# Feed-forward as two layers per token half, the second also in seven half products

## The chip, the cores and the metric

The kernel runs on one core of one Trainium2 chip. The metric is the device time of one execution in microseconds (us); several executions are given by their median. The engines are named as the profile names them: PE (matmuls) with its weight loads PEld, DVE, ACT, POOL, and SP, whose queue issues most of the DMAs.

## The reference

One decoder layer on 2048 tokens of width 1024: a token mixer (stick-breaking attention and gated DeltaNet, unchanged here) and then a feed-forward part, all in float32:

```python
h = rmsnorm(x, norm_mlp[l]) * (1.0 + sc_m) + sh_m
x = x + g_m * (jnp.square(jax.nn.relu(h @ w_ff1[l])) @ w_ff2[l])
```

w_ff1 is 1024 x 4096, w_ff2 is 4096 x 1024. The scale, the shift and the gate g_m come from a conditioning vector.

## The kernel before

Everything is kept transposed: features on the 128 partitions, tokens in the free dimension. Each float32 product is made of three matmuls in the reduced type fp32r: an operand is split into a high part (a rounding copy on ACT) and a low part (operand minus high part, a subtraction on DVE or POOL), and high x high, high x low and low x high are summed in PSUM. A left operand's parts are called wh and wl (swh and swl in the first feed-forward layer), with three buffers each.

After the mixer, project_out makes the mixer's output product for 512 tokens (a chunk) at a time and writes x1, the residual stream, to DRAM; outs(2), then outs(1, 0) are the last calls. load_h(1) stands between them: it loads x1 of the second half of the tokens (chunks 2 and 3), normalizes and modulates it, and makes the right operands of the first feed-forward layer. These lie in pool fb on the right side of SBUF, four tiles of each kind. load_h(0) makes those of the other half.

The first layer, ff1(hf, g), makes 256 features (group g of 16) for one half of the tokens (1024 tokens, hf). It is a 2 x 2 block product over halves of the input features, of the 256 features and of the 1024 tokens, done by seven block products in place of eight (Strassen's scheme in Winograd's form). Each of the seven has 4 matmul steps of 128 input features and three matmuls per step: 84 in all. summed makes the four sums or differences of weight blocks on POOL, product splits a left operand and multiplies, take copies a partial result from PSUM (ACT), add adds one from PSUM (DVE) and applies relu and the square (ACT). load_h makes the sums on the right side once per half of the tokens, into the tiles b0, b12, b56 and b43 (bh for high, bl for low parts).

split then splits the features, and ff2(hf, g, hid, ys) multiplies them with the 256 matching rows of w_ff2, in the plain way: 8 output tiles x 2 feature tiles x 2 token chunks x 3 = 96 matmuls. Each of the 16 PSUM tiles of 128x512 is evicted by one scalar_tensor_tensor (L1181) that multiplies with g_m and adds to the accumulator ys in SBUF. So the loop alternates: ff1 of group g+1 is issued ahead of ff2 of group g. A loop turn is 84 + 96 matmuls, and there are 32 turns (2 halves x 16 groups). At the last group but one of the first half, load_h(0) is issued with high priority.

PSUM has 8 banks in this stage: four with tag f1 for the first layer and four with tag f2 for the second. All engines run their instructions in a fixed order, which a planner sets beforehand: it simulates the engines, starts what is ready by priority, and gives buffers of a pool to whichever tile asks first in that simulation. tc.high_priority moves instructions ahead. DMAs of the SP queue are issued in that fixed order too, and one that waits for its buffer holds back those behind it.

Of the kernel before, what the change touches and what calls it, by code (L numbers as in the profile page):

```python
# [56 lines left out]
def tile_hybrid_layer(  # L57
# [74 lines left out]
    if True:  # L132
# [883 lines left out]
        ADD, SUB = ALU.add, ALU.subtract  # L1016
        fb = right.enter_context(tc.tile_pool(name="fb", bufs=4, side="right", reuse_waits="tile"))

        def load_h(hf, pair, rs):

            out = [[] for _ in range(7)]
            for k in range(4):
                bt = {}
                for j, shape in (("0", [P, CH]), ("12", b2_), ("56", b2_), ("43", b2_)):
                    bt[j] = [fb.tile(shape, F32R, tag=f"b{i}{j}", name=f"b{i}{hf}_{k}{j}") for i in "hl"]
                b = []
                for i in range(2):
                    kk = k + 4 * i
                    x = pair(f"fx{hf}_{kk}")
                    for n in range(2):  # L1030
                        nc.sync.dma_start(x[:, n], x1_d[2 * hf + n][:, kk, :])
                    for n in range(2):
                        V.tensor_tensor(x[:, n], x[:, n], rs[n], ALU.mult)  # L1033
                    A.activation(x, x, AF.Identity, scale=g2[:, kk:kk + 1], bias=mods[:, 24 + kk:25 + kk])
                    b.append(x)

                def parts2(j, x):
                    hi, lo = bt[j]
                    A.copy(hi, x)
                    lo_part(lo, x, hi)  # L1040

                x1, x2 = b
                parts2("0", x1[:, 0])
                parts2("12", x2)
                G.tensor_tensor(x1[:, 0], x1[:, 1], x1[:, 0], SUB)
                G.tensor_tensor(x1[:, 1], x2[:, 1], x1[:, 1], SUB)
                parts2("56", x1)
                G.tensor_tensor(x2[:, 1], x2[:, 1], x1[:, 0], SUB)
                G.tensor_tensor(x2[:, 0], x2[:, 1], x2[:, 0], SUB)  # L1049
                parts2("43", x2)  # L1050
                out[0].append(bt["0"])
                for j, (key, i) in enumerate((("12", 0), ("12", 1), ("43", 0), ("56", 0), ("43", 1), ("56", 1))):
                    out[j + 1].append([t[:, i] for t in bt[key]])
            return out
# [235 lines left out]
```

## Time and profile before

| what | value |
|---|---|
| runs, median (lowest to highest) | 2884.83 us (2874.47 to 2891.14) |
| the profiled execution | 2880.04 us, its span 2878.2 us |
| PE busy, share of the span | 93% |
| DVE, ACT, POOL busy | 67%, 44%, 30% |
| mean granted clock | 0.966 of full speed |

The busy times are sums over a span with several stages: mixer first, feed-forward from about 1520 us to the end. Line numbers (L1176) are those of the kernel printed above; names such as swh are the tiles' names without their numbers. PE's matmuls overlap in the records, so one is shown longer (about 0.39 us) than the distance from start to start.

### The profile page before, as it was taken

The page shows a single profiled execution, that of the slowest core. Times are in us where ns is not written, and L with a number is a line of the kernel's source. Part 1 is how long each engine was busy: PE and PEld are TensorE (multiplying, and loading weights), DVE is VectorE, ACT ScalarE, POOL GpSimd, SP SyncE. Part 2 cuts the span into 40 slices and gives each one's busy share as a digit, 9 for nine tenths or more (in the row PEclk, how much of TensorE's full clock was granted, in tenths as well). Part 3 has the DMA queues.
Part 4 walks back from the last instruction along what each step waited for, and adds up shares of the span by engine and source line. Part 5 has one row for each costly group of instructions (what it writes and reads, how often), then busy time and mean ns, then how long its engine had stood idle before and what let it go on. Part 6 is the DMA issues. An engine that isn't in the chain of part 4 may idle for free.

```text
span 2878.2 us, 37573 instructions
## 1 busy us (share of the span) xinstructions
PE 2684.7 (93%) x13044; PEld 2144.3 (75%) x13044; DVE 1933.6 (67%) x4355; ACT 1264.1 (44%) x2488; POOL 873.7 (30%) x686
## 2 busy tenths in 40 slices
PE   3998889789999899989989999999998999999999
PEld 2786667667787677866667888888876888888887
DVE  7487889695775968676685555556568556555555
ACT  4553444444553456535454433343345443344332
POOL 3333313241322523132264222222235222222221
PEclk9998999899999999999999999999999999999999
DMA  7443675343344444336463111111125111111012
GB/s 249 158 149 107 195 240 193 93 130 130 120 149 126 153 135 151 116 88 194 137 199 131 59 46 43 59 59 40 49 86 177 59 59 35 54 59 59 30 59 88
DMA packets 184612, 321.17 MB, mean 112 GB/s; under 512 B 22216, under 2 KB 69320, under 8 KB 180296
## 3 DMA queue, kind: packets, MB, share of 16 engines
q1 hardware_dynamic: 167368, 291.20, 31.4%
q10 hardware_dynamic: 17024, 27.27, 2.6%
q8 instruction: 110, 1.80, 0.3%
q14 instruction: 110, 0.90, 0.1%
HBM read 263.22 MB, written 55.18 MB: 111 GB/s over the span
## 4 chain that ended last, share of the span: by engine, by line
PE 45%; DVE 2%; issue 1%; POOL 1%; DMA 1%; ACT 1%; SPq 0%; ACTq 0%; POOLq 0%; DVEq 0%
PE f L1176 8%; PE f L1177 8%; PE f L1178 8%; PE f L1117 7%; PE f L1118 7%; PE f L1119 7%; DMA wa<-in_w_ff_dram 1%; PE mmo L194 0%; PE mmo L193 0%; PE mmo L192 0%; DVE fx L1033 0%; DVE bl L130 0%; DMA fx<-x_d 0%; POOL fx L1049 0%; DVE swl L1111 0%
## 5 line engine op out<-in xcount | busy, mean ns | idle before, releaser
L1181 DVE SCALAR_TENSOR_TENSOR y<-f,mods,y 128x512 f32<-128x512 f32 x512 | 363.5, 745 | 248.3 <-PE f L1178 248.1
L1176 PE MATMUL f<-hidh,wh 128*128 128x512 f32 x1024 | 400.1, 392 | 7.2 <-DVE y L1181 7.1
L1177 PE MATMUL f<-hidl,wh 128*128 128x512 f32 x1024 | 401.2, 392 | 3.2 <-POOL hidl L1159 3.2
L1178 PE MATMUL f<-hidh,wl 128*128 128x512 f32 x1024 | 380.6, 391 | 0.8 <-POOL wl L173 0.8
L1117 PE MATMUL f<-bh,swh 128*128 128x512 f32 x896 | 354.9, 396 | 4.2 <-ACT swh L1110 2.9
L1118 PE MATMUL f<-bl,swh 128*128 128x512 f32 x896 | 354.1, 395 | 0.0
L1119 PE MATMUL f<-bh,swl 128*128 128x512 f32 x896 | 348.5, 395 | 0.8 <-DVE swl L1111 0.5
L1176 PEld LDWEIGHTS f<-hidh,wh 128*128 128x128 f32 x1024 | 192.7, 188 | 54.3 <-DVE y L1181 12.1
L1177 PEld LDWEIGHTS f<-hidl,wh 128*128 128x128 f32 x1024 | 193.1, 189 | 45.0 <-POOL hidl L1159 4.4
L1178 PEld LDWEIGHTS f<-hidh,wl 128*128 128x128 f32 x1024 | 193.0, 189 | 42.6 <-POOL wl L173 1.2
L172 ACT CAST wh<-ws 128x512 fp32r<-128x512 f32 x128 | 79.5, 621 | 299.3 <-PE f L1177 243.0
L1159 POOL TENSOR_TENSOR hidl<-t,hidh 128x512 fp32r<-128x512 f32 x64 | 102.1, 1595 | 335.0 <-ACT hidh L1158 315.4
L1117 PEld LDWEIGHTS f<-bh,swh 128*128 128x128 f32 x896 | 168.3, 188 | 47.4 <-ACT swh L1110 4.9
L1119 PEld LDWEIGHTS f<-bh,swl 128*128 128x128 f32 x896 | 168.1, 188 | 43.7 <-DVE swl L1111 2.5
L1118 PEld LDWEIGHTS f<-bl,swh 128*128 128x128 f32 x896 | 168.1, 188 | 40.8 <-issue 0.2
L1103 POOL TENSOR_TENSOR sws<-wa 128x512 f32<-128x512 f32 x64 | 88.5, 1383 | 311.1 <-DVE wl L173 285.2
L1110 ACT CAST swh<-wa 128x512 fp32r<-128x512 f32 x96 | 59.4, 622 | 263.7 <-PE f L1118 258.1
L1131 DVE TENSOR_TENSOR t<-t,f 128x512 f32<-128x512 f32 x128 | 87.3, 683 | 120.6 <-PE f L1119 86.9
L1111 DVE TENSOR_TENSOR swl<-sws,swh 128x512 fp32r<-128x512 f32 x128 | 144.3, 1128 | 25.1 <-ACT swh L1110 25.1
L1111 DVE TENSOR_TENSOR swl<-wa,swh 128x512 fp32r<-128x512 f32 x96 | 86.3, 902 | 98.6 <-ACT swh L1110 98.6
L679 DVE SCALAR_TENSOR_TENSOR cv<-raw,vecs,cv 128x256 f32<-128x256 f32 x288 | 136.8, 522 | 16.2 <-ACT cv L675 15.8
L173 POOL TENSOR_TENSOR wl<-ws,wh 128x512 fp32r<-128x512 f32 x52 | 67.8, 1304 | 247.6 <-ACT wh L172 247.1
(344 smaller groups left out, 6341.9 us busy)
## 6 DMA issues: line engine op xcount, KB each, us to landing
wa<-in_w_ff_dram SPq DMA_DIRECT2D x32, 1024.0 KB
ws<-in_w_ff_dram SPq DMA_DIRECT2D x128, 256.0 KB
wada<-in_w_ada_dram SPq DMA_DIRECT2D x48, 512.0 KB
wso<-in_w_out_dram SPq DMA_DIRECT2D x64, 256.0 KB
raw_d<-ev ACTq DMA_DIRECT2D x48, 256.0 KB
x<-in_xc_dram SPq DMA_DIRECT2D x40, 256.0 KB
wsk<-in_w_m_dram SPq DMA_DIRECT2D x32, 256.0 KB
wsv<-in_w_m_dram SPq DMA_DIRECT2D x32, 256.0 KB
```

The source lines that it names most:

```text
L679: V.scalar_tensor_tensor(y[:, h, :], raw[:, h, m:m + HALF], vecs[:, w0:w0 + 1], y[:, h, :], ALU.mult, ALU.add)
L1103: G.tensor_tensor(t, x, y, op)
L1111: V.tensor_tensor(wl, x, wh.bitcast(F32), SUB)
L1117: T.matmul(ps, lhsT=wh[:, k, :], rhs=ah, start=first and k == 0, stop=False, skip_group_check=True)
L1118: T.matmul(ps, lhsT=wh[:, k, :], rhs=al, start=False, stop=False, skip_group_check=True)
L1119: T.matmul(ps, lhsT=wl[:, k, :], rhs=ah, start=False, stop=stop and k == 3, skip_group_check=True)
L1131: V.tensor_tensor(t, t, ps, op)
L1159: (G if i % 2 else V).tensor_tensor(hl, x, hh.bitcast(F32), SUB)
L1176: T.matmul(ps[n], lhsT=wh[:, s], rhs=ah, start=j == 0, stop=False)
L1177: T.matmul(ps[n], lhsT=wh[:, s], rhs=al, start=False, stop=False)
L1178: T.matmul(ps[n], lhsT=wl[:, s], rhs=ah, start=False, stop=j == 1)
L1181: V.scalar_tensor_tensor(ys[m][:, cs], ps[n], mods[:, 40 + m:41 + m], ys[m][:, cs], ALU.mult, ALU.add)
```

## The change

- The two layers are separated. For each half of the tokens all 16 groups of ff1 run first; then ff2 runs in four steps q, each with four groups' features (1024 features).
- ff1 takes the order of products 0, 4, 5, 2, 6, 3, 1. Its four feature blocks and the three further sums and differences that the right side of a seven-product scheme wants are made on POOL (four more instructions per group) and written to DRAM, seven tiles of 128x512 per group (h_d). Its PSUM tags alternate (f0, f1) from group to group.
- ff2 is a 2 x 2 block product over halves of 256 features, of the 1024 outputs and of the 1024 tokens, with seven products too. For each product, four groups are summed in PSUM, four output tiles side by side, before they are evicted. Its right operands are loaded from h_d into the tiles of pool fb, unsplit, into the place of the low part, and split there by in_parts (ACT copy, DVE subtraction). Its left operands come by the same routines as in ff1 (blocks, lefts, left); every fourth low part is made on POOL.
- Weights of both layers are laid out as four blocks of 128x512 per group by the host, loaded one by one into pool fu, and combined in place; the same buffers take the feature blocks t11 to t22 (tags A11 to A22), and tag S takes the sums.
- load_h works on single 128x512 tiles, makes the "12" tiles in a second loop for which it loads and normalizes half of x1 again, and for the second call stands behind ff2 of the first half, without high priority. For the first call its tiles come from the tags nxs (2 buffers) and nx (3 buffers, which project_out uses).

The diff, cut to what the text speaks of:

```diff
+        def right_tile(j, name):
+            return [fb.tile([P, CH] if j == "0" else b2_, F32R, tag=f"b{i}{j}", name=f"b{i}{name}") for i in "hl"]
+        def in_parts(t, eng=V):
+            hi, lo = t
+            A.copy(hi, lo.bitcast(F32))
+            eng.tensor_tensor(lo, lo.bitcast(F32), hi.bitcast(F32), SUB)
...
+            for k in range(4):
+                x11, x12 = [norm(k, 0, n, "ws") for n in range(2)]
+                x21, x22 = [norm(k, 1, n, "S") for n in range(2)]
+                split_right(bt[k]["0"], x11)
+                G.tensor_tensor(x11, x12, x11, SUB)
+                G.tensor_tensor(x12, x22, x12, SUB)
+                split_right(bt[k]["56"], x11, x12)
+                G.tensor_tensor(x22, x22, x11, SUB)
+                G.tensor_tensor(x21, x22, x21, SUB)
+                split_right(bt[k]["43"], x21, x22)
+            for k in range(4):
+                split_right(bt[k]["12"], *[norm(k, 1, n, "S") for n in range(2)])
...
-        bs = load_h(1, lambda n: np_.tile(b2_, F32, tag="nxs", name=n, bufs=2), rs1)
+        bs = load_h(1, lambda tag, n: np_.tile([P, CH], F32, tag="nxs" if tag == "ws" else "nx", name=n,
+                                               bufs=2 if tag == "ws" else 3), rs1)
...
-        fa = ffp("fa", 1)
-        fh = ffp("fh", 4)
-        fx = ffp("fx", 4)
+        fu = ffp("fu", 4)
...
+        def left(x, name, share):
...
+            with tc.high_priority():
+                A.copy(wh, x)
+                (G if share and nl[0] % share == 0 else V).tensor_tensor(wl, x, wh.bitcast(F32), SUB)
...
+            def get(j):
+                x = (lambda: a11, lambda: a12, lambda: comb(s, a12, s, SUB), lambda: a22, lambda: comb(s, a21, a22, ADD),
+                     lambda: comb(s, s, a11, SUB), lambda: comb(a11, a11, a21, SUB))[j]()
+                return left(x, f"{name}_{j}", share)
...
+            put(2, t22)
+            put(1, t21)
+            put(0, t11)
+            G.tensor_tensor(t1, t12, t11, SUB)
+            put(4, t1)
+            G.tensor_tensor(t12, t22, t12, SUB)
+            put(6, t12)
+            G.tensor_tensor(t2, t22, t1, SUB)
+            put(5, t2)
+            G.tensor_tensor(t4, t2, t21, SUB)
+            put(3, t4)
...
+            order = ((0, a), (4, 1 - a), (5, a), (2, 1 - a), (6, a), (1, 1 - a), (3, a))
+            if q == 3 and hf:
+                order = order[:4] + ((3, 1 - a), (6, a), (1, 1 - a))
...
+                for i, g in enumerate(gs):
+                    if key not in bt[i]:
+                        bt[i][key] = right_tile(key, f"2{hf}_{g}{key}")
+                        js = [n for n in range(7) if RIGHT[n][0] == key]
+                        for n in js:
+                            nc.sync.dma_start(place(bt[i], n)[1].bitcast(F32), h_d[hf][g][:, n, :])
+                        in_parts(bt[i][key])
...
+                for i in range(4):
+                    wh, wl = get[i](j)
+                    ah, al = place(bt[i], j)
+                    for m in range(4):
+                        s = slice(m * P, (m + 1) * P)
+                        ps = banks[ch][m]
+                        T.matmul(ps, lhsT=wh[:, s], rhs=ah, start=first and i == 0, stop=False, skip_group_check=True)
+                        T.matmul(ps, lhsT=wh[:, s], rhs=al, start=False, stop=False, skip_group_check=True)
+                        T.matmul(ps, lhsT=wl[:, s], rhs=ah, start=False, stop=i == 3, skip_group_check=True)
+                with tc.high_priority():
+                    for m in range(4):
+                        for m0, cs in dst[j]:
+                            y = ys[m0 + m][:, cs:cs + CH]
+                            gt = ngate[:, m0 + m:m0 + m + 1] if j == 3 else mods[:, 40 + m0 + m:41 + m0 + m]
+                            V.scalar_tensor_tensor(y, banks[ch][m], gt, y, ALU.mult, ALU.add)
...
+        for hf in (1, 0):
+            for g in range(NG):
+                ff1(hf, g, bs)
...
+            for q in range(4):
+                ff2(hf, q, ys)
+            if hf:
+                bs = load_h(0, lambda tag, n: wp.tile([P, CH], F32, tag=tag, name=n) if tag == "ws" else unit(tag, n),
+                            [accs2[0], accs2[1]])
```

## Rows read from the trace of the kernel before

**Rows 1.** The page: busy time per engine, and data moved in 40 equal slices.
```profile
PE 2684.7 (93%) x13044; PEld 2144.3 (75%) x13044; DVE 1933.6 (67%) x4355; ACT 1264.1 (44%) x2488; POOL 873.7 (30%) x686
...
GB/s 249 158 149 107 195 240 193 93 130 130 120 149 126 153 135 151 116 88 194 137 199 131 59 46 43 59 59 40 49 86 177 59 59 35 54 59 59 30 59 88
```
**Rows 2.** Busy time by stretch: one loop turn, and the change of halves.
```profile
core 0: us, PE busy (x) PEld busy (x) DVE busy (x) ACT busy (x) POOL busy (x), PEclk, DMA share, GB/s
...
2146.40:2211.00 64.60, 53.50 (x208) 40.50 (x207) 58.52 (x68) 33.48 (x43) 40.62 (x24) 0.92 0.45 156
...
1880.80:1922.22 41.42, 41.42 (x182) 33.73 (x180) 24.46 (x33) 15.86 (x28) 9.34 (x8) 1.00 0.15 51
```
**Rows 3.** Waits of PE from 1650 us on: total us, times, longest.
```profile
PE f L1176 <- DVE y L1181: 7.1, 5, 2.9
```
**Rows 4.** Timeline of PE (start, us): where blocks of either layer begin, last matmul.
```profile
1519.83 0.50 PE L1117 MATMUL f<-bh,swh 128*128 128x512 f32 x1 [2.31 <-ACT swh L1110]
...
1564.14 0.39 PE L1176 MATMUL f<-hidh,wh 128*128 128x512 f32 x1
...
1880.80 0.39 PE L1117 MATMUL f<-bh,swh 128*128 128x512 f32 x1
...
1897.60 0.39 PE L1176 MATMUL f<-hidh,wh 128*128 128x512 f32 x1
...
1922.22 0.39 PE L1117 MATMUL f<-bh,swh 128*128 128x512 f32 x1
...
2146.41 0.39 PE L1176 MATMUL f<-hidh,wh 128*128 128x512 f32 x1
...
2248.30 0.39 PE L1176 MATMUL f<-hidh,wh 128*128 128x512 f32 x1
...
2873.24 0.39 PE L1178 MATMUL f<-hidh,wl 128*128 128x512 f32 x1
```
**Rows 5.** Groups by line and shape, 1650 to 2878 us: busy us, mean ns; idle.
```profile
L1181 DVE SCALAR_TENSOR_TENSOR y<-f,mods,y 128x512 f32<-128x512 f32 x480 | 340.7, 745 | 230.7 <-PE f L1178 230.5
L1111 DVE TENSOR_TENSOR swl<-sws,swh 128x512 fp32r<-128x512 f32 x112 | 127.7, 1140 | 17.8 <-ACT swh L1110 17.8
L1131 DVE TENSOR_TENSOR t<-t,f 128x512 f32<-128x512 f32 x112 | 76.5, 683 | 107.7 <-PE f L1119 77.0 <-ACT t L1127 30.7
...
L130 DVE TENSOR_TENSOR bl<-fx,bh 128x1024 fp32r<-128x1024 f32 x12 | 18.0, 1507 | 1.6 <-ACT bh L1039 1.6
...
L1132 ACT ACTIVATE t<-t 128x512 f32<-128x512 f32 x113 | 71.4, 632 | 71.4 <-DVE t L1131 71.4
```
**Rows 6.** Timeline of DVE and POOL (start, us, then engine and line).
```profile
1909.26 1.29 POOL L1103 TENSOR_TENSOR sws<-wa 128x512 f32<-128x512 f32 x1 [8.75 <-DVE wl L173]
1909.76 1.34 DVE L1111 TENSOR_TENSOR swl<-wa,swh 128x512 fp32r<-128x512 f32 x1
...
1921.64 0.68 DVE L1111 TENSOR_TENSOR swl<-sws,swh 128x512 fp32r<-128x512 f32 x1
1922.12 1.36 POOL L1159 TENSOR_TENSOR hidl<-t,hidh 128x512 fp32r<-128x512 f32 x1 [11.57 <-ACT hidh L1158]
1922.25 1.40 DVE L1181 SCALAR_TENSOR_TENSOR y<-f,mods,y 128x512 f32<-128x512 f32 x2
1923.57 0.68 DVE L1159 TENSOR_TENSOR hidl<-t,hidh 128x512 fp32r<-128x512 f32 x1
...
2158.63 1.21 DVE L130 TENSOR_TENSOR bl<-fx,bh 128x1024 fp32r<-128x1024 f32 x1
...
2175.05 1.73 POOL L1049 TENSOR_TENSOR fx<-fx 128x512 f32<-128x512 f32 x1
```
**Rows 7.** Chain that ended last: transfers, start, us until landed.
```profile
1456.29 3.56 DMA x_d<-x
...
1514.28 4.81 DMA wa<-in_w_ff_dram
```
**Rows 8.** Tile fx, 1330 to 1560 us: min/median/max ns, first and last start.
```profile
L130 DVE TENSOR_TENSOR bl<-fx,bh x16: 677/1284/2315, 1445.1 to 1529.2; 128x1024 fp32r<-128x1024 f32 x12, 128x512 fp32r<-128x512 f32 x4
```

More of the change, by code (lines that the diff above doesn't have):

```diff
@@ L1016, in tile_hybrid_layer @@
         ADD, SUB = ALU.add, ALU.subtract
+        RIGHT = (("0", None), ("12", 0), ("12", 1), ("43", 0), ("56", 0), ("43", 1), ("56", 1))
         fb = right.enter_context(tc.tile_pool(name="fb", bufs=4, side="right", reuse_waits="tile"))
-        def load_h(hf, pair, rs):
-            out = [[] for _ in range(7)]
-            for k in range(4):
[L1023 to L1054, printed above, removed]
@@ L1106, in product @@
[L1106 to L1111 removed]
+            get = lefts(blocks(lambda i: w_ff1[g, i], "1" + nm), unit("S", "s1" + nm), nm)
+            def product(j, ps=None, stop=True):
+                wh, wl = get(j)
@@ L1119, in product @@
-                    T.matmul(ps, lhsT=wl[:, k, :], rhs=ah, start=False, stop=stop and k == 3, skip_group_check=True)
-                return ps
-            ts = [fx.tile(b2_, F32, tag="t", name=f"t{nm}_{i}") for i in range(2)]
-            t11, t12, t21, t22 = ts[0][:, 0], ts[0][:, 1], ts[1][:, 0], ts[1][:, 1]
+                    s = slice(k * P, (k + 1) * P)
+                    T.matmul(ps, lhsT=wh[:, s], rhs=ah, start=first and k == 0, stop=False, skip_group_check=True)
+                    T.matmul(ps, lhsT=wh[:, s], rhs=al, start=False, stop=False, skip_group_check=True)
@@ L1125, in take @@
+                    T.matmul(ps, lhsT=wl[:, s], rhs=ah, start=False, stop=stop and k == 3, skip_group_check=True)
+                return ps
+            t11, t12, t21, t22 = [unit(t, f"t{nm}_{i}") for i, t in enumerate(AB)]
             def take(t, ps):
@@ L1144, in ff1 @@
[L1144 removed]
+            product(2, v)
+            add(t12, v)
+            product(6, u)
             take(t21, u)
             add(t22, u)
[L1147 to L1161 removed]
@@ L1186, in tile_hybrid_layer @@
-        work = [(hf, g) for hf in (1, 0) for g in range(NG)]
-        hid = split(1, 0, ff1(1, 0, bs))
-        for i, (hf, g) in enumerate(work):
-            if g == 0:
-                ys = load_y(hf)
-            switch = g == NG - 1
-            if switch:
-                ff2(hf, g, hid, ys)
-            t = ff1(*work[i + 1], bs) if i + 1 < len(work) else None
-            if g == NG - 2 and hf:
-                with tc.high_priority():
-                    bs = load_h(0, lambda n: fx.tile(b2_, F32, tag="t", name=n), [accs2[0], accs2[1]])
-            if not switch:
-                ff2(hf, g, hid, ys)
-            if t is not None:
-                hid = split(*work[i + 1], t)
-            if i == 0:
-                for f in rstd([accs2[0]], "2", "20", pf, "f2"):
-                    f()
+            add(t21, product(3), SUB)
@@ new lines, in ff1, with put @@
+            add(t11, product(1))
+            out = h_d[hf][g]
+            t1, t2, t4 = [unit("S", f"T{nm}_{i}") for i in range(3)]
+            def put(j, t):
+                nc.sync.dma_start(out[:, j, :], t)
+            put(2, t22)
[7 more added lines that the diff above has]
+            put(5, t2)
```

141 lines of the change are left out of this document (77 added, 64 removed).

## The prediction

> **What bounds the kernel now.** I read the page first: TensorE is busy for 93% of the span, and its neighbours are far below that [rows 1]. A busy share says nothing of a stage, so the next view is the table of stretches: in one turn of the feed-forward loop, 41.42 us, PE is busy for all 41.42 us at full granted clock (1.00, the 2.4 GHz level), with DVE at 24.46 us and POOL at 9.34 us [rows 2]. The chain of waits agrees: from 1650 us on, all waits of PE are a handful, the longest sort 7.1 us in total [rows 3]. So this stage goes as fast as its matmuls issue, and taking matmuls away pays until another engine is late.
>
> The timeline of PE gives the price of one. Between 1880.80 and 1897.60 us stand 72 products of the first layer: 16.80 / 72 = 0.2333 us each. A turn from 1880.80 to 1922.22 us holds 84 of the first layer and 96 of the second, so the second costs (41.42 - 84 x 0.2333) / 96 = 0.2273 us [rows 4]. I could not find what makes the difference; the first layer's right operands lie in pool fb, the second's in fh.
>
> The same view gives what the stage loses today. It runs from 1519.83 us to the end of its last matmul, about 2873.5 us: 1353.6 us [rows 4]. 32 turns of 41.42 us are 1325.4 us, so 28.2 us are lost. At the start, 168 products take 1564.14 - 1519.83 = 44.3 us in place of 39.2 us: 5.1 us. At the change of halves, 2146.41 to 2248.30 us, 192 products of the second layer and 168 of the first take 101.9 us in place of 82.8 us: 19.0 us [rows 4]; there the clock falls to a mean of 0.92 and DVE is busy for 58.5 of 64.6 us [rows 2], because load_h runs beside everything else. Some 4 us are left over, and a tail of under 5 us (2873.5 to 2878.2 us).
>
> **Matmuls.** Before: 32 x (84 + 96) = 5760. After, the first layer keeps 32 x 84 = 2688; the second has, for each of 2 halves and 4 steps q, 7 products x 4 groups x 4 output tiles x 3 = 336, so 2688 in place of 3072: 384 fewer. The right operand of the second layer now also comes from fb. At the first layer's pitch the stage holds 5376 x 0.2333 = 1254.3 us, 71.1 us less than now; at the second layer's present pitch for its half, 1238.1 us, 87.3 us less. I take 0.2333, since fb is the nearest row, and keep the other end.
>
> **What the other engines get.** Prices: a DVE subtraction of two SBUF tiles starts 0.61 us before the next instruction (1921.64 to 1922.25 us), one of 1024 columns takes 1.21 us, a PSUM eviction (0.745 us by its own row [rows 5]) repeats every 0.66 us (two from 1922.25 to 1923.57 us), a POOL combination takes 1.29 us when alone and 1.73 us when DVE is in its way [rows 6]. Means are higher, 1140 ns for the subtraction of combined weights and 1507 ns for the wide one [rows 5], and the timeline shows why. POOL combines from 1909.26 to 1910.55 us; the subtraction that DVE began at 1909.76 us takes 1.34 us and so ends 0.55 us after POOL. The pair of evictions at 1922.25 us takes 1.40 us with POOL at work from 1922.12 us [rows 6]: undisturbed. So two-tile subtractions and POOL shut each other out, and evictions do not.
>
> Second layer, one step q of 336 x 0.2333 = 78.4 us. DVE: of 28 left splits 21 on DVE, 21 x 0.61 = 12.8; right splits of 4 groups, 4 x 0.61 + 12 x 1.21 = 17.0; evictions 8 x 4 x 0.66 = 21.1; sum 50.9 us. POOL: 16 combinations and 7 splits, 23 x 1.29 = 29.7 us. What must not overlap is 12.8 + 17.0 + 29.7 = 59.5 us, 76% of the step. ACT: 28 left copies and the same 28 units of right copies at about 0.63, 35 us. All fit, and the order leaves slack: the same bank is needed again two products (22 us) later with another product between, so its 4 to 8 evictions (2.6 to 5.3 us) have 11 us; left splits run up to three ahead (three buffers of wh and wl). I put 8 us for all eight steps, bounds 0 and 30.
>
> First layer, one group of 19.6 us: DVE 7 x 0.61 + 4 x 0.6 = 6.7, POOL 4 combinations of weights and 4 new ones of features, 8 x 1.29 = 10.3, ACT 18 x 0.63 = 11.3. That fits too, but the chain is tight. Product 5 of the next group needs its combination after split 4, which needs a buffer that product 3 frees 2.8 us before the group ends (T). Reckoned from prices: split 4 until T - 1.5, combination until T - 0.2, split 5 until T + 1.1, combination 2 until T + 2.4 at best and about T + 5 if POOL holds two feature combinations ahead of it (these wait for the last eviction, 0.68 us, and two activations, 0.63 us each, so they begin at T + 2) [rows 5, 6]; split 2 is ready by T + 6.3; needed at T + 8.4. I put 5 us in all, bounds 0 and 30.
>
> Features through DRAM: 7 x 256 KB written and read per group, 117 MB in all. With weights that is 2.75 MB per 19.6 us, 140 GB/s; the loop now moves 59 GB/s in most slices, and other slices reach 240 [rows 1]. It is hidden by bandwidth; where a tile comes free late, latency shows.
>
> **The changes of stage.** (a) Start. load_h(1) ends now at 1529 us, about 10 us after the first product [rows 4, 8]. It gets 8 more loads, normalizations and activations, an estimate of 4 x 5 us (a load of 3.6 us as in [rows 7] and two short operations) through three buffers (nx) that it newly shares with project_out. Waiting loads sit in SP's queue, with weights behind them. PE may take other products first (product 2 alone needs all of "12"). 20 us, bounds 5 and 45. (b) First to second layer, twice: the last group of ff2's first step takes the buffer of t11, which comes free by an add and two activations (1.95 us) and a store (3.56 us); reload 3.6 to 4.8 us [rows 7], split 1.2 us: 10.3 to 11.6 us against 8.4 us until its product. 4 us each, bounds 0 and 10. (c) Second layer back to first: load_h(0) has 24 multiplications and 28 splits (52 x 0.61 = 31.7 us) and 16 combinations (20.6 us), 52 us on the shut-out pair; the present one has 16 + 12 wide + 4 narrow and the same combinations, 47 us, and loses 19.0 us. But most of the new one waits for the last products of ff2 to free fb. 25 us, bounds 10 and 45. The rest stays at 4 us, and the tail as it is.
>
> Sum: 20 + 8 + 25 + 4 + 5 + 8 = 70 us lost in place of 28.2. Stage 1254.3 + 70 = 1324 us against 1353.6: 29 us less. The profiled execution took 2880.0 us (span 2878.2), within the runs' 2874 to 2891 (median 2884.8): 2880 - 29 = **2851 us**.
>
> The Trainium skill, SBUF — State Buffer, "Who interferes with whom", says that a VectorE instruction with two SBUF inputs and a GpSimd instruction that reads SBUF exclude each other for the whole instruction; the trace agrees, by the 1.34 us row above. It speaks against this change, which gives POOL 16 x 8 + 4 x 23 = 220 instructions per half of the tokens where it has about 120 now (7.5 per turn). By the rule alone, with 59.5 us of 78.4 us on the pair, the sum stands; with everything in a row it is the second rival's.
>
> **Rivals.** Cover holds: the changes of stage cost no more than now, 28 us. Stage 1282 us, or 1266 at the faster pitch: 2809 or 2793 us. For it: PE loses nothing in 30 of 32 turns [rows 2, 3]. Against: two more changes of stage, and load_h with later buffers. Chance 0.20.
>
> The lock binds in the second layer: each POOL instruction finds DVE with a subtraction next, so nothing overlaps and DVE needs 50.9 + 29.7 = 80.6 us a step, 2.2 over PE's, 18 us in all; with PE stalls of a few us at each bank handover, 40 us. 2851 - 8 + 18 to 40 = 2861 to 2883 us. For it: the means of 1140 and 1507 ns [rows 5]; against: evictions overlap with POOL. Chance 0.12.
>
> The other side, slower: in the first layer POOL's queue has all four feature combinations ahead of combination 2 of the next group. Begun at T + 2, with 1.73 us each when DVE shuts them out, they end at T + 8.9, the combination at T + 10.6, split 2 at T + 12.4: 4 us late in each of 30 groups, 120 us: 2851 - 5 + 120 = 2966 us. It decides from about 1 us per group (29 / 30). For it: POOL's order is fixed ahead of time and it waits in order. Against: the combination has high priority and is ready first by my reckoning. Chance 0.13.
>
> **How the numbers follow.** Forecast 0.55, alone 2815 to 2890. A measurement can tell about 0.5%, 14 us: faster is below about 2866 in this frame. The forecast gives 0.47 faster, 0.05 same, 0.03 slower; the second rival 0.06 and 0.06: faster 0.73, same 0.11, slower 0.16. The range, 2795 to 2900, leaves out the slow rival and the best corner.
>
> **What would show it.** Right: 5376 products of about 0.233 us; within a step of ff2 and a group of ff1 no wait of PE over 1 us; losses in four clusters, at the start, twice at ff1 to ff2 with A11 and wh last, once around load_h(0) with bl last. Wrong: a wait of PE for swh or swl after POOL's combination in each group of ff1; waits for y's evictions through ff2; POOL or DVE near 100% there; SP waiting long with weights behind; PE idle over 45 us ahead of the first product.

## The result, and the profile after

The changed kernel takes **3234.25 us** (median, 3229.92 to 3235.81) against 2887.98 us (2874.47 to 2893.77) for the kernel before on the same chips: ratio **1.122**, 95% interval 1.119 to 1.125. The prediction was 2851 us, 1.3% faster; its range ended at 2900 us.

The page of the profiled execution (3235.3 us, span 3233.5), first the busy times, then the granted clock in 40 slices and one group of instructions (busy us, mean ns; idle before, releaser):

```profile
PE 2707.4 (84%) x12660; PEld 2131.2 (66%) x12660; DVE 1950.2 (60%) x4296; ACT 1393.9 (43%) x2640; POOL 1157.9 (36%) x882
...
PEclk9999899899999999967988888899988888889999
...
L1157 PE MATMUL f<-bh,swh 128*128 128x512 f32 x896 | 388.9, 434 | 215.2 <-ACT swh L1126 214.5
```

There are 384 fewer matmuls than in [rows 1], as reckoned, and PE falls from 93% to 84% of a longer span. No other engine is near its limit: DVE 60%, ACT 43%, POOL 36%. The clock, at 9 in most slices elsewhere, is 8 through both first layers, and 6 and 7 from 1374 to 1536 us, where project_out waits. L1157 is the first matmul on the left high part in ff1, and PE idles 214.5 us ahead of it.

Waits of PE, from 1500 us on (total us, times, longest), and the longest one ahead of that:

```profile
PE f L1157 <- ACT swh L1126: 214.5, 32, 23.2
PE f L1241 <- ACT swh L1126: 33.4, 7, 15.2
PE f L1243 <- DVE swl L1127: 22.4, 14, 2.8
```

```profile
PE mmo L192 <- ACT hm L883: 62.1, 2, 60.0
```

In [rows 3] the same view of before has 7.1 us as its largest entry. mmo is project_out's product, ahead of the feed-forward; L1241 to L1243 are ff2's matmuls. The timeline of PE gives the four blocks (ff1, ff2 of one half, ff1, ff2 of the other) and the last matmul:

```profile
1595.69 0.50 PE L1157 MATMUL f<-bh,swh 128*128 128x512 f32 x1 [2.38 <-ACT swh L1126]
...
2048.47 0.40 PE L1241 MATMUL f<-bh,swh 128*128 128x512 f32 x1
...
2403.42 0.39 PE L1157 MATMUL f<-bh,swh 128*128 128x512 f32 x1
...
2880.30 0.40 PE L1241 MATMUL f<-bh,swh 128*128 128x512 f32 x1
...
3228.95 0.40 PE L1243 MATMUL f<-bh,swl 128*128 128x512 f32 x1
```

Each block has 1344 matmuls, 313.6 us at the prediction's 0.2333 us. The blocks take 452.8, 355.0, 476.9 and 348.7 us, and begin 75.9 us later than in [rows 4]. So 75.9 + 139.2 + 41.4 + 163.3 + 35.1 = 454.8 us are lost, where 70 were forecast; the difference, 385 us, is the error of the prediction.

### One group of the first layer

Nearly all joints between two groups look alike (27 waits of 6.4 us). PE and POOL around one of the joints:

```profile
2597.08 0.39 PE L1159 MATMUL f<-bh,swl 128*128 128x512 f32 x1
2603.90 0.80 PE L1157 MATMUL f<-bh,swh 128*128 128x512 f32 x1 [6.43 <-ACT swh L1126]
```

```profile
2580.10 1.29 POOL L1136 TENSOR_TENSOR s<-A,s 128x512 f32<-128x512 f32 x1 [0.63 <-DVE swl L1127]
2596.80 1.28 POOL L1195 TENSOR_TENSOR T<-t,t 128x512 f32<-128x512 f32 x1 [15.40 <-ACT t L1172]
2598.16 1.26 POOL L1197 TENSOR_TENSOR t<-t,t 128x512 f32<-128x512 f32 x1
2599.38 1.26 POOL L1199 TENSOR_TENSOR T<-t,T 128x512 f32<-128x512 f32 x1
2600.72 1.26 POOL L1201 TENSOR_TENSOR T<-T,t 128x512 f32<-128x512 f32 x1
2601.93 1.26 POOL L1136 TENSOR_TENSOR s<-A,A 128x512 f32<-128x512 f32 x1
2604.65 1.27 POOL L1136 TENSOR_TENSOR s<-s,A 128x512 f32<-128x512 f32 x1 [1.45 <-DVE swl L1127]
```

The last matmul of product 0 of the next group starts at 2597.08 us; product 4 needs its left operand, combination 4 (s<-A,A). POOL had stood idle for 15.4 us, with the weights in place (the last load for them was issued by 2576 us), but its next instructions were the four feature combinations (L1195 to L1201), which wait for the last activation. Combination 4 comes fifth. Then ACT and DVE split it, and PE goes on after a wait of 6.4 us.

Busy time by stretch, the clock in the column after POOL's: one such period, then the first matmuls after the wait, then later ones.

```profile
2575.10:2603.90 28.80, 21.39 (x84) 16.78 (x84) 7.87 (x12) 11.96 (x20) 10.38 (x9) 0.86 0.33 111
...
2604.00:2610.00 6.00, 6.00 (x14) 4.65 (x15) 1.93 (x3) 1.40 (x3) 3.83 (x3) 0.50 0.34 124
2611.00:2624.00 13.00, 13.00 (x57) 10.47 (x56) 4.28 (x8) 6.63 (x11) 0.00 (x0) 1.00 0.06 23
```

A period holds 84 matmuls and takes 28.8 us in place of 19.6. After the wait PE runs at 0.50, that is 1.2 of 2.4 GHz: 14 matmuls in 6.00 us, 0.43 us each in place of 0.23.

### The profile page after: what moved, and what is told of

Same layout as the page of the kernel before. It is cut to its first block, busy times and chain, and to the rows that moved or that the text cites. A ratio compares the mean times of both kernels' runs of the same rounds, so it can differ in the third digit from the quotient of the medians.

```text
span 3233.5 us, 38722 instructions
## 1 busy us (share of the span) xinstructions
PE 2707.4 (84%) x12660; PEld 2131.2 (66%) x12660; DVE 1950.2 (60%) x4296; ACT 1393.9 (43%) x2640; POOL 1157.9 (36%) x882
## 5 line engine op out<-in xcount | busy, mean ns | idle before, releaser
L1157 PE MATMUL f<-bh,swh 128*128 128x512 f32 x896 | 388.9, 434 | 215.2 <-ACT swh L1126 214.5
L1127 DVE TENSOR_TENSOR swl<-s,swh 128x512 fp32r<-128x512 f32 x168 | 169.0, 1007 | 408.9 <-ACT swh L1126 405.6
L1241 PE MATMUL f<-bh,swh 128*128 128x512 f32 x896 | 361.4, 403 | 33.7 <-ACT swh L1126 33.4
L1158 PE MATMUL f<-bl,swh 128*128 128x512 f32 x896 | 379.7, 424 | 3.2 <-DVE bl L130 3.2
L1159 PE MATMUL f<-bh,swl 128*128 128x512 f32 x896 | 372.1, 421 | 0.7 <-DVE swl L1127 0.7
L1157 PEld LDWEIGHTS f<-bh,swh 128*128 128x128 f32 x896 | 185.1, 207 | 273.1 <-ACT swh L1126 228.8
L1242 PE MATMUL f<-bl,swh 128*128 128x512 f32 x896 | 359.9, 402 | 0.0
L1243 PE MATMUL f<-bh,swl 128*128 128x512 f32 x896 | 319.5, 402 | 22.5 <-DVE swl L1127 22.4
L1127 DVE TENSOR_TENSOR swl<-A,swh 128x512 fp32r<-128x512 f32 x224 | 173.8, 777 | 186.8 <-ACT swh L1126 185.0
L1195 POOL TENSOR_TENSOR T<-t,t 128x512 f32<-128x512 f32 x32 | 41.9, 1310 | 515.8 <-ACT t L1172 477.7
L1241 PEld LDWEIGHTS f<-bh,swh 128*128 128x128 f32 x896 | 172.0, 192 | 79.4 <-ACT swh L1126 37.6
L1158 PEld LDWEIGHTS f<-bl,swh 128*128 128x128 f32 x896 | 186.2, 208 | 48.0 <-DVE bl L130 3.6
L1159 PEld LDWEIGHTS f<-bh,swl 128*128 128x128 f32 x896 | 183.0, 204 | 52.2 <-DVE swl L1127 8.3
L1243 PEld LDWEIGHTS f<-bh,swl 128*128 128x128 f32 x896 | 169.5, 191 | 70.1 <-DVE swl L1127 29.5
L1032 DVE TENSOR_TENSOR bl<-bl,bh 128x1024 fp32r<-128x1024 f32 (+1 forms) x128 | 179.0, 1420 | 56.2 <-ACT bh L1031 56.2
L1242 PEld LDWEIGHTS f<-bl,swh 128*128 128x128 f32 x896 | 172.0, 192 | 41.8
L1249 DVE SCALAR_TENSOR_TENSOR y<-f,mods,y 128x512 f32<-128x512 f32 x224 | 153.5, 741 | 3.6 <-PE f L1243 3.5
```

What stands on the lines that cost most here:

```text
L1032: eng.tensor_tensor(lo, lo.bitcast(F32), hi.bitcast(F32), SUB)
L1127: (G if share and nl[0] % share == 0 else V).tensor_tensor(wl, x, wh.bitcast(F32), SUB)
L1157: T.matmul(ps, lhsT=wh[:, s], rhs=ah, start=first and k == 0, stop=False, skip_group_check=True)
L1158: T.matmul(ps, lhsT=wh[:, s], rhs=al, start=False, stop=False, skip_group_check=True)
L1159: T.matmul(ps, lhsT=wl[:, s], rhs=ah, start=False, stop=stop and k == 3, skip_group_check=True)
L1241: T.matmul(ps, lhsT=wh[:, s], rhs=ah, start=first and i == 0, stop=False, skip_group_check=True)
```

## The experiments

**The theories.** A, order: a tile's tag gives out its buffers in an order that the program's text fixes, so what the text has later stands behind. In ff1, s of group g + 1 shares tag S with the T tiles of group g; project_out's mx shares tag nx with load_h(1)'s tiles; the first s of the second half shares S with load_h(0)'s tiles. Its rivals: B, SP's queue holds weights behind the feature stores; C, POOL has too much work; D, the new load_h is simply longer; O, the buffers are too few. Theories of single runs (L, M, Q, R) are told with them. Runs without a range after the time are single executions; one kernel's executions differ by up to 22 us below, so a difference of 10 us between two such runs shows nothing. The expectations are those written before each run; the kernel before took 2887.72 us beside the first four runs.

### T tiles in another tag

```diff
-            t1, t2, t4 = [unit("S", f"T{nm}_{i}") for i in range(3)]
+            t1, t2, t4 = [wp.tile([P, CH], F32, tag="ws", name=f"T{nm}_{i}") for i in range(3)]
```

> The changed kernel with one edit: the three new feature sums of a group (T) take their buffers from another tag, ws of pool wp, which lies idle in this stage, in place of tag S, which they share with the weight combinations s. All work stays. Theory A (buffers of one tag are given out in the order of the text, so that s of the next group is asked for behind the three T, and POOL's fixed order has its combination behind them): PE's wait of 6.4 us per group of the first layer goes, with the slow clock behind it, some 8.7 us in each of 30 groups: about 2975 us (2950 to 3005). Rival B (weights of the next group come late, because SP holds them behind stores of features that are not ready): 3234 within 15. Rival C (POOL has too much to do in a group, whatever the order): 3234 within 15.

Measured: **2985.56 us**, 249 us less, with the same work on every engine (below, this run is T in ws). POOL's timeline around one joint:

```profile
1700.74 1.29 POOL L1136 TENSOR_TENSOR s<-A,s 128x512 f32<-128x512 f32 x1 [0.63 <-DVE swl L1127]
1701.98 1.30 POOL L1197 TENSOR_TENSOR t<-t,t 128x512 f32<-128x512 f32 x1
1703.24 1.74 POOL L1199 TENSOR_TENSOR T<-t,T 128x512 f32<-128x512 f32 x1
1705.06 1.62 POOL L1201 TENSOR_TENSOR T<-T,t 128x512 f32<-128x512 f32 x1
1709.83 1.29 POOL L1136 TENSOR_TENSOR s<-A,A 128x512 f32<-128x512 f32 x1 [3.14 <-DMA A<-in_w_ff_dram]
...
1718.49 1.31 POOL L1195 TENSOR_TENSOR T<-t,t 128x512 f32<-128x512 f32 x1
```

Combination 4 of a group (1709.83 us) now comes 8.7 us ahead of the first feature combination of the group before it (1718.49 us), and only combination 2 (s<-A,s) stands among those. The first ff1 block takes 329.0 us in place of 452.8, the second 355.2 in place of 476.9: 245.5 us over 30 joints, 8.2 us each, of which 6.4 are the wait; the rest goes with the lower clock. B and C fall: SP's stores and POOL's work are the same.

### The sum written earlier, T tiles left where they were

```diff
+            if g + 1 < NG:
+                ready.append(ask(hf, g + 1, True))   # combination 4 of group g + 1 is written out here
             out = h_d[hf][g]
             t1, t2, t4 = [unit("S", f"T{nm}_{i}") for i in range(3)]
```

> The changed kernel with the T tiles still in tag S; only combination 4 of the next group is written out ahead of the T combinations in the program's text, so its first writing instruction comes before theirs. The run with T in ws (2985.6 us) took T out of the tag, which left s more buffers and changed the order as well; here the number of buffers is as in the changed kernel. Theory A (order: a tag's buffers are given in the order of the first writing instructions, and so the combination stood behind the four T's): 2985 us (2960 to 3010). Theory O (occupancy: four buffers of S are too few for s and three T's, the combination waits for one to come free): the waits of 6.4 us stay, 3234 us (3200 to 3250).

Measured: **2992.39 us** (before beside it 2883.82). The run above had also left s more buffers; here it has as many as in the changed kernel, and the waits are gone all the same. O falls: it is the order. (The edit moves the group's four weight requests ahead as well; in the changed kernel they were in place long before, as said above.) The description ahead of the prediction has the planner give a buffer to whichever tile asks first in its simulation, and combination 4 was ready first; these two runs show that the place in the text of the first writing instruction decided. The waits of PE for swh in ff1 (L1165 is its first matmul here):

```profile
PE f L1165 <- ACT swh L1126: 33.3, 7, 23.6
```

### Feature combinations on DVE

```diff
-            G.tensor_tensor(t1, t12, t11, SUB)
+            V.tensor_tensor(t1, t12, t11, SUB)
```
(and so for the other three)

> The changed kernel with one edit: the four feature sums of a group run on DVE in place of POOL; tags and buffers stay. Theory A, in the form that it is the place in POOL's queue that holds the combination: the wait goes, about 2975 us (2950 to 3010). Theory A, in the form that s waits for a buffer that is really occupied until a T is stored: the wait stays, 3234 within 20. Rival B: 3234 within 20. Rival C: about 2975 us.

Measured: **3092.33 us**, between both forms and within no range that was expected. POOL is free of the T's, but now the left split of combination 4 stands behind them on DVE:

```profile
1767.89 0.69 DVE L1195 TENSOR_TENSOR T<-t,t 128x512 f32<-128x512 f32 x1 [1.36 <-ACT t L1172]
...
1769.94 0.69 DVE L1201 TENSOR_TENSOR T<-T,t 128x512 f32<-128x512 f32 x1
1770.55 0.69 DVE L1127 TENSOR_TENSOR swl<-s,swh 128x512 fp32r<-128x512 f32 x1
```

The queue moved, at 0.69 us an instruction in place of 1.3. PE waits 1.19 us for swh and 0.76 us for swl at most joints. The 0.76 us are DVE's; the 1.19 us are ACT's order, in which the cast of combination 4 (1769.13 us) stands behind the copy of product 0 (1768.65 us), though POOL had stood idle for 16.0 us behind the combination. Yet the first ff1 block takes 380.4 us, 51 more than with T in ws. In it the waits that the timeline names come to 33.3 us; the starts of matmuls, less these waits and 0.2333 us each, leave another 33.5 us. The clock after the short wait:

```profile
1769.80:1775.00 5.20, 4.43 (x13) 3.21 (x14) 2.62 (x4) 0.62 (x1) 2.98 (x3) 0.74 0.97 314
```

### Stores on ACT's queue

```diff
-                nc.sync.dma_start(out[:, j, :], t)
+                nc.scalar.dma_start(out[:, j, :], t)
```

> The changed kernel with one edit: the seven feature stores of a group are issued from ACT's queue in place of SP's, so that no weight load stands behind one. Theory A: PE's wait of 6.4 us per group stays, 3234 us within 25 (issuing costs ACT some time). Rival B: the wait goes, about 2975 us. Rival C: 3234 within 25.

Measured: **3245.95 us**, and PE waits for swh in ff1 as before the edit:

```profile
PE f L1157 <- ACT swh L1126: 214.4, 31, 23.2
```

SP is free of the stores, and nothing is gained. B falls a second time, as the cause of these waits.

### The first load as it was, and the new one with a tag of its own

```diff
-        bs = load_h(1, lambda tag, n: np_.tile([P, CH], F32, tag="nxs" if tag == "ws" else "nx", ...), rs1)
+        bs = load_first(1, lambda n: np_.tile(b2_, F32, tag="nxs", name=n, bufs=2), rs1)   # load_h of before
```

> The changed kernel with one part undone: the first call of load_h is as it was before the change (pairs of tiles in tag nxs, no second loop, nothing from tag nx). Theory A (project_out's loads ask for nx behind the 16 tiles of load_h(1), so PE stands still for 60 us before outs(1)): the wait of 60 us goes, the first product of the feed-forward part moves from 1595.7 us to about 1525, and the time to about 3165 us (3150 to 3180). Rival D (load_h simply has more loads, normalizations and port conflicts, and these delay the start): the old form still makes 28 units of splits and 16 combinations, so less than 25 us come back, 3210 to 3235.

Measured: **3175.26 us**, 59 us less; the first feed-forward product starts at 1536.05 us in place of 1595.69. That takes away both the shared tag and the second read of x21 and x22. The next run (on top of T in ws) keeps the second read and takes away the shared tag (load_h(1) then has four half tiles of nxs, in place of two tiles of nxs and three of nx):

```diff
+        def half(tag, n):                      # halves of pair tiles in tag nxs; nx is left to project_out
+            if not pair:
+                pair.append(np_.tile(b2_, F32, tag="nxs", name=n, bufs=2))
+                return pair[0][:, 0]
+            return pair.pop()[:, 1]
+        bs = load_h(1, half, rs1)
```

> T in ws, and load_h(1) in its new form (x21 and x22 read twice), with all its tiles in tag nxs in place of nxs and nx: project_out's mx has nx for itself. Theory A (mx stands behind load_h(1)'s tiles because they share a tag): the wait of 60 us before project_out's first product goes, the first feed-forward product starts at 1530 to 1550 us, 2930 us (2915 to 2950). Theory D (the new load itself, 24 loads and 28 splits ahead on SP, ACT and DVE, is what project_out stands behind): 30 us of wait or more stay, 2955 us or more.

Measured: **2937.91 us**, 48 us under the run with T in ws; the first product starts at 1533.82 us in place of 1585.12. The waits of PE around there, before 1600 us:

```profile
PE f L1163 <- ACT swh L1132: 23.5, 2, 20.7
...
PE mmo L192 <- ACT hm L883: 2.0, 2, 1.1
```

project_out's wait of 60 us for hm is gone; 20.7 us stand ahead of the first feed-forward product in its place. So D falls for most of the start's loss: the shared tag made it.

### Three edits at once

T in ws, the old first load, and this, to have the second half's first weights and s ahead of load_h(0):

```diff
             if hf:
+                ready.append(ask(0, 0))
                 bs = load_h(0, ...)
```

> Three edits on the changed kernel: the T tiles in the tag ws, load_h(1) in its old form, and weights and s of the first group of the second half asked for ahead of load_h(0). From the run with T in ws (2985.6 us): the first feed-forward product starts at about 1536 us as with the old first load, in place of 1585.1, so 49 us less; the wait of 23.8 us after the change from the second layer back to the first falls to 3 us or less, with its stretch at the lower clock some 22 us less. Theory A (a tile is handed out in the order of the text within its tag, so what is asked for later stands behind): 2915 us (2895 to 2935), still slower than before or level with it. Theory D (load_h(0) itself is that long, the weights are not the point): the 23.8 us stay, 2935 us or more.

Measured: **2928.73 us** (2925.99 to 2935.09) against 2882.82 for before; ratio 1.0171, interval 1.014 to 1.020. The start came (1526.59 us); the change back to ff1 did not: its wait is 22.9 us (23.2 after the change). To ask for s early is not enough, since the instruction that first writes s still stood behind load_h(0) in the text. POOL stands idle for 9.37 us ahead of it, until a split of load_h(0):

```profile
2241.71 1.26 POOL L1172 TENSOR_TENSOR s<-A,A 128x512 f32<-128x512 f32 x1 [9.37 <-DVE bl L130]
```

POOL's own order has nothing in the way by then. What that split can hold up is a buffer: load_h(0)'s second loop has its tiles in tag S, and each is free when DVE has split it. The trace names the split alone; the rest is read from the text.

### Buffers that come free earlier at the change of layer

Base: three edits at once, as for the two runs that follow.

```diff
-            t11, t12, t21, t22 = [unit(t, f"t{nm}_{i}") for i, t in enumerate(AB)]
+            last = g == NG - 1
+            t11, t12, t21, t22 = [unit("S" if last and t != "A12" else t, f"t{nm}_{i}") for i, t in enumerate(AB)]
```

> As three_fixes, and in the last group of each first layer t11, t21 and t22 lie in tag S, so that no weight tile of the second layer's first step takes a buffer that the last feature combination holds. Theory R (the wait of 17 to 18 us in product 0 of the second layer is for the fourth A11, whose buffer is held by t11 until combination T1 and the store are done): both waits fall to 4 us or less, 27 to 33 us below three_fixes, about 2883 us. Theory M (the change of layer is bound by transfers: 13.6 MB in 37 us, DMA 99% busy): waits of 12 to 18 us stay, within 8 us of three_fixes.

Measured: **2923.94 us** (2920.73 to 2938.0), ratio to before 1.0164, interval 1.0126 to 1.0202. The wait of 18.6 us in product 0 is gone, so it was for the buffer (R); the 27 to 33 us that R expected did not come, and 4.8 us between the medians are within the spread. For product 4, next in the order, now waits, at 1877.25 and 1886.15 us:

```profile
1877.25 0.79 PE L1284 MATMUL f<-bh,swh 128*128 128x512 f32 x1 [4.03 <-ACT swh L1162]
...
1886.15 1.22 PE L1286 MATMUL f<-bh,swl 128*128 128x512 f32 x2 [5.30 <-DVE swl L1163]
```

Here POOL's combinations stand between and behind the last T's (1866.92 to 1884.41 us). The last group of ff1 got a new wait of 3.9 us: t11, t21 and t22 share tag S with s, and combination 4 (1833.45 us) stands behind a T (1832.21 us) again. ff2 is 8.5 and 6.8 us shorter than in the run with three edits, ff1 4.8 and 9.4 us longer.

### Left splits of the second layer on DVE; right subtraction left out

```diff
-                get.append(lefts(blocks(...), unit("S", f"s2{hf}_{g}"), f"2{hf}_{g}", 4))
+                get.append(lefts(blocks(...), unit("S", f"s2{hf}_{g}"), f"2{hf}_{g}", 0))
```

> As three_fixes, with all left splits of the second layer on DVE: POOL has 16 instructions per step in place of 23, DVE 7 more. Theory L (POOL and DVE shut each other out, and this is the second layer's loss of 23 us per half beyond its first wait): the sum on the pair falls from 59.5 to 54.7 us per step, 10 to 20 us less than three_fixes. Theory Q (DVE's own queue: left splits stand behind right splits and evictions): 0 to 15 us more.

Measured: **2894.94 us**, 34 us less than with three edits. In its place, the other run, which leaves the right low parts out:

```diff
-                        in_parts(bt[i][key])
+                        A.copy(bt[i][key][0], bt[i][key][1].bitcast(F32))
```

> As three_fixes, but the second layer's right low parts are not computed: the subtraction of in_parts is left out (its low operand is the whole feature tile), 16 instructions and some 17 us of DVE less per step. If the right splits on DVE are what the second layer's left splits wait for (Q, and L in another form): the loss of 23 us per half beyond the first wait falls to 8 us or less, some 30 us below three_fixes. If the loss is the clock or transfers: within 8 us of three_fixes.

Measured: **2886.31 us**, 42 us less than with three edits. Waits of PE in the second layer for swl, three edits first, then with the left splits on DVE:

```profile
PE f L1285 <- DVE swl L1163: 23.7, 16, 2.8
...
PE f L1285 <- POOL swl L1163: 0.8, 1, 0.8
```

```profile
PE f L1283 <- ACT swh L1162: 37.0, 2, 18.8
...
PE f L1285 <- DVE swl L1163: 1.5, 4, 0.5
```

And DVE's groups in the second layer of the first half (busy us, mean ns), three edits, then left splits on DVE:

```profile
L1032 DVE TENSOR_TENSOR bl<-bl,bh 128x1024 fp32r<-128x1024 f32 x36 | 49.5, 1378 | 18.9 <-ACT bh L1031 18.9
L1163 DVE TENSOR_TENSOR swl<-A,swh 128x512 fp32r<-128x512 f32 x43 | 41.3, 963 | 32.4 <-ACT swh L1162 32.4
```

```profile
L1032 DVE TENSOR_TENSOR bl<-bl,bh 128x1024 fp32r<-128x1024 f32 x36 | 45.9, 1288 | 8.8 <-ACT bh L1031 8.7
L1163 DVE TENSOR_TENSOR swl<-A,swh 128x512 fp32r<-128x512 f32 x58 | 44.1, 765 | 28.8 <-ACT swh L1162 28.8
```

PE's waits were for splits made on DVE, and they vanish when DVE gets seven more of them per step and POOL seven fewer: DVE was not short of time, it was held up. Its subtractions get shorter (963 to 765 ns, 1378 to 1288 ns) as POOL leaves. One of the waits with three edits, 2.8 us until 2836.15 us, had this ahead of it:

```profile
2832.10 2.32 DVE L1032 TENSOR_TENSOR bl<-bl,bh 128x1024 fp32r<-128x1024 f32 x1
2833.29 2.26 POOL L1163 TENSOR_TENSOR swl<-A,swh 128x512 fp32r<-128x512 f32 x1
2834.35 1.75 DVE L1163 TENSOR_TENSOR swl<-A,swh 128x512 fp32r<-128x512 f32 x1
```

A right split takes 2.32 us (1.21 undisturbed), the left split behind it 1.75 us (0.68), with a left split on POOL across both. Seven of the twelve waits over 0.6 us for a split on DVE have such a stretched split (15.2 of 21.8 us); in the other five the left split stands behind undisturbed ones in DVE's order, and these waits vanish as well. That speaks for theory L, POOL and DVE shutting each other out, with more than the 10 to 20 us it expected; Q, which expected more time, falls. But the edit changed the order on both engines too, and these runs do not part that from the exclusion. Leaving out the right subtraction ends the same waits (1.1 us are left), and the second layer is as long as with the left splits on DVE: 337.3 and 335.7 us, 336.3 and 336.8 us there. The 8.6 us between these two single runs lie outside the second layer, 5.9 of them ahead of the first feed-forward product, which neither edit touches: taking work off DVE gave nothing there beyond what its left splits had given.

### All together

Late buffers and left splits on DVE, and:

```diff
+            pre = {4: comb(s, a21, a22, ADD)} if early else {}      # early: first group of the second half
...
-                split_right(bt[k]["12"], *[norm(k, 1, n, "S") for n in range(2)])
+                split_right(bt[k]["12"], *[norm(k, 1, n, ("ws", "S")[n]) for n in range(2)])
...
+            E = V if g >= NG - 2 else G        # and E for G in the four T combinations
```

> late_buffers and left_splits_on_dve together (T in ws, old first load, t11, t21 and t22 of the last group in S, left splits of the second layer on DVE), with three more edits: T of the last two groups on DVE, so that POOL's combinations at the change of layer stand behind nothing; combination 4 of the first group of the second half written out ahead of load_h(0), since the order printed for three_fixes shows that a buffer goes by the first writing instruction, not by the request; the second read of x21 in ws, that of x22 in S. From left_splits_on_dve (2894.9 us): the wait of 18.8 and 18.2 us in product 0 of the second layer falls to 5 us or less (theory R with POOL's queue clear), 25 to 32 us less; the 23 us after the second layer fall to 13 to 18 us, since load_h(0) goes on until about 30 us after the change whatever is asked early, 5 to 10 us less. Forecast 2860 us (2845 to 2880), 0.8% under before. If the transfers of the change of layer (some 13 MB in 37 us) bind, the waits only move to product 4 and 5: 2885 us or more, level with before.

Measured: **2882.87 us** (2867.63 to 2889.48) against 2880.78; ratio 0.9997, interval 0.9981 to 1.0014: level with before, and 23 us over the forecast. Waits of PE from 1520 us on:

```profile
PE f L1201 <- ACT swh L1162: 23.1, 9, 7.5
PE f L1289 <- DVE swl L1163: 12.8, 7, 3.8
PE f L1201 <- ACT bh L1038: 7.7, 3, 5.5
PE f L1287 <- ACT swh L1162: 6.4, 2, 3.6
```

The waits in product 0 at the change to ff2 are gone; 2.9, 3.6 and 2.3 us, and 3.6 and 3.8 us, stand in the products after it. That is the place, and nearly the time, that the expectation's other case had (transfers bind), but the rows speak for another cause. Busy time at the first of the two changes (DVE in the third pair of columns; the last two are the DMA engines' busy share and GB/s), and one combination ahead of the wait of 2.9 us:

```profile
1868.00:1885.00 17.00, 14.66 (x63) 11.46 (x61) 16.25 (x20) 14.19 (x20) 4.79 (x3) 1.00 1.05 393
1885.00:1908.30 23.30, 16.64 (x56) 12.27 (x56) 23.30 (x19) 9.55 (x15) 17.75 (x11) 0.85 0.35 111
...
1880.21 3.39 POOL L1172 TENSOR_TENSOR s<-s,A 128x512 f32<-128x512 f32 x1 [22.62 <-DVE swl L1163]
```

The burst of transfers is over at 1885 us; after it the DMA engines are busy 0.35 of the time. DVE, which now has the T's and all left splits, is busy all of the 23.3 us in which the waits of 3.6 and 2.3 us lie, and both end with a split of DVE; ahead of the wait of 2.9 us DVE is busy too, and POOL takes 3.39 us for a combination of 1.29. No run took work off DVE in this version.

The change back to ff1 has no wait for s any more, but 5.5 and 1.9 us for bh and 2.6 and 1.8 us for bl of load_h(0) itself. Its first group takes 44.9 us in place of 49.9 with three edits, so the order gave 5.0 us back. The block is 354.5 us long all the same, 2.7 more than with three edits: its last group takes 25.9 us in place of 21.2 (a wait of 4.0 us, new with the late buffers), its fifth 27.8 in place of 24.9. The fifth group is long in both halves (27.7 and 27.8 us, the groups beside it 19.7): SP's queue has the 16 loads of the accumulators ys between its weights there, and POOL stands idle for 11.8 us ahead of combination 4, until a weight lands. So rival B has a place, one group in sixteen, and no run moved it. No version beat the kernel before.

## Why the prediction was wrong, step by step

What each term of the sum was, and what the traces give for it (us lost; the waits for the three changes of layer are named waits, the lower clock after them is in the layers' own rows):

| term | forecast (bounds) | changed kernel | all together |
|---|---|---|---|
| start: delay of the first product | 20 (5 to 45) | 75.9 | 11.8 |
| ff1, 32 groups, with the rest | 9 (4 to 34) | 275.4 | 52.3 |
| ff1 to ff2, two waits | 8 (0 to 20) | 29.9 | 16.1 |
| ff2, eight steps | 8 (0 to 30) | 46.5 | 14.9 |
| ff2 to ff1 | 25 (10 to 45) | 27.1 | 11.8 |
| sum | 70 | 454.8 | 106.9 |

**Matmuls and their pitch: right.** 5376 products, 0.2333 us apart wherever PE is neither waiting nor at the lower clock, 71 us less than before. By the last column 106.9 us are lost in place of 28.2, 78.7 more: that is why all together is level.

**The first layer: the step that failed.** Of the 385 us, 266 are here: 275.4 us lost in place of 9. The prices were right: the T's were to begin at T + 2 and began 2.3 us after the group's end, at 1.26 to 1.28 us each (1.29 reckoned). The position was wrong. The prediction put two to four feature combinations ahead of combination 2, needed at T + 8.4, and took combination 4, needed at T + 2.8, for done. The slower rival had the right mechanism, POOL's fixed order with the T's ahead, and "the combination has high priority" stood against it; but s and the T's both lie in tag S, and priority does not pass a buffer that is not yet given. With combination 4 fifth, 2.3 + 4 x 1.28 + 1.26 + 0.62 us of cast are T + 9.3 against T + 2.8: 6.5 us, and 6.4 was measured. The rival's 4 us x 30 = 120 us was 8.2 us x 30 = 245.5 us: the combination was needed two products earlier than the one it reckoned with, and the clock was not in it.

**Start: mechanism missed.** The prediction saw that nx is newly shared and that loads would queue, and priced the load's length. What stood behind was not the first product but project_out's operands, 60.0 us; with the tag apart 48 to 59 us come back. The upper bound, 45, was itself built on the load alone.

**ff1 to ff2: right place, short price.** 15.2 and 14.7 us in place of 4 each, over the bound of 10. The buffer of t11 was named; its three steps were priced as if nothing else ran. In the changed kernel, from the end of the first block at 2048.47 us, the add and two activations end at 2054.15 us, 5.7 us in place of 1.95, since splits and casts for ff2 stand between them; the first of the last four weight loads goes out at 2061.07 us, 6.9 us for a store in place of 3.56; and the cast of its tile begins at 2071.57 us, 10.5 us in place of 3.6 to 4.8, behind a full queue (below). With the cast that is 23.7 us against the 8.4 at which the product needs it. (That this load is the one into t11's buffer is read from the order of the text.) With T in ws POOL adds to it: T1, which reads t11 too, runs at 1923.44 us, behind three combinations from 1917.50 us that had stood 13.2 us for weights. late_buffers shows the buffer as the cause in product 0.

**ff2 steady: near the second rival's size, not by its mechanism.** 46.5 us against 8, and against its 18 to 40; some 26 us are waits, the rest lies in no wait, part of it in the lower clock after the two waits above. The rival had DVE busy for more than the whole step; it was busy for 207.5 of 290 us (2100 to 2390 us). The sum, 59.5 of 78.4 us on the shut-out pair, said that everything fits; but PE waits by the product. A right split of 1.2 us that POOL stretches to 2.3 us stands ahead of a left split that is due (five of eleven waits over 0.6 us have a stretched left split, 12.0 of 21.0 us), and slack in another product does not help. 76% of a step on two engines that shut each other out was no slack to be put at 8 us.

**ff2 to ff1: right in size.** 27.1 us against 25. 23.2 of them are a wait for s behind load_h(0), a cause that the prediction did not have; but with s written early load_h(0) itself is late, as argued, and the first group still takes 25 us more than the others (44.9 and 19.7 us).

**The range.** It left out the slow rival and took every term's likely value: its own upper bounds add up to 174 us, 2955 us by the same sum, against a range that ended at 2900. The four terms that failed are all places where a tile newly shares buffers or an engine's order with another: S, nx, A11, and POOL with DVE.

## What to carry to other kernels

When a change moves tiles into shared buffers, list for each tag who writes it first and in which order the text has these writes: a planner that gives buffers in that order puts the later one behind the earlier one's wait, whatever its priority, and one edit of a tag (249 us) or of the place of one instruction (242 us) was worth that here. Price a wait by the product that needs it, not by the sum over the step, and add the lower clock after it. And a saving in matmuls that is spread over a stage (71 us) should be set against each new change of layer (some 10 to 30 us each) before anything else.

## What the runs showed of the hardware

After a wait of 6.4 us PE's next 14 matmuls ran at a granted clock of 0.50; after a wait of 1.19 us, with another of 0.76 us in it, a stretch of 5.2 us had 0.74, with eight matmuls 0.43 us apart. In the first ff1 block of the changed kernel, starts less named waits less 0.2333 us a matmul leave 47 us beside 92 us of waits; with the T's on DVE, whose waits are mostly under 2 us, they leave 33.5 us beside 33.3. That short waits cost half as much again, or as much again, had not been in the sum.

At the change to ff2 (T in ws, 1905 to 1942 us) the DMA engines are full (busy share 1.00), which the prediction's mean of 140 GB/s had hidden (its 2.75 MB per group count 1024 x 1024 bytes each; counted as in the profile it is 2.88 MB and 147 GB/s):

```profile
DMA packets 7474, 13.62 MB, mean 368 GB/s; under 512 B 827, under 2 KB 827, under 8 KB 7473
```

In the last version the burst at this change is as dense (393 GB/s) and ends at 1885 us, ahead of two of the three waits that are left there.
